# Hybrid encoder block: the first norm's second row tile in two parts, most rows scaled on GpSimd, and TensorE in a given order until the first half of the tokens is through

## The chip, the cores and the metric

The kernel runs on one core of a Trainium2 chip. The metric is the device time of one execution in microseconds (us), the median of three runs. The names of the engines in the profile: PE is TensorE (matmuls; PEld its weight loads), DVE is VectorE, ACT is ScalarE, POOL is GpSimd, SP is SyncE, which issues most of the loads. An `ACTq` or `SPq` is the part of an engine that issues DMAs.

## The reference

One layer of a streaming encoder over 512 tokens of 1024 features, in float32. What matters here is its beginning:

```python
def rmsnorm(x, g):
    var = jnp.mean(x * x, axis=-1, keepdims=True)
    return x * lax.rsqrt(var + EPS) * g

xn = rmsnorm(h, norm_mix_g)
u = xn @ w_in                               # 1024 x 7168
q, k, v, xr, gr, ga, gb = split(u)          # 1024 columns each
ya = chunked_band_attention(q, k, v) @ w_attn_out
xc = causal_depthwise_conv(xr)              # then the RG-LRU, times gelu(gr)
yb = ... @ w_rnn_out
mix = (sigmoid(ga + b) * ya + sigmoid(gb + b) * yb) @ w_o
h = h + mix;  h = h + SwiGLU(rmsnorm(h));  out = rmsnorm(h)
```

So every projection of `u` reads the normed rows `xn`, with tokens on the free axis of TensorE and features on the partitions.

## The kernel before

**Numbers.** TensorE multiplies in a format of reduced precision. To keep float32's precision, every operand is split into a high part and a low part (what is left of it), and a product is three matmuls into the same bank (`mm3`): high by high (L80), weights high by x low (L81), weights low by x high (L82). The order's names read out<-in; `whl_xr_0` holds the high and low parts of the weights of chunk xr, feature blocks 0 to 3, and `whl_xr_4` those of blocks 4 to 7. The high part of a weight tile is made by ACT (L672, L86), the low part by VectorE (L673, L87), from a raw tile (`raw_xr`) that SP loads. The tiles `whl` come from a pool of four buffers, so the tile of the fifth, `whl_ga_0`, takes the buffer of `whl_xr_0` when TensorE has read that for the last time.

**The first norm.** The 512 tokens lie in four row tiles x0 to x3 of 128 tokens. x0 and x1 are "half 0", x2 and x3 "half 1". For each half, `rstds` makes the sum of squares of the first tile on ACT, and of the second tile half on ACT (`low`, the columns 0 to 511) and half on VectorE (`high`, 512 to 1023), then the root on ACT and the reciprocal on VectorE. `scaled_first` and `scaled_rest` scale the rows into `xs_mix`: the low columns of both tiles on VectorE, later the high columns of the first tile on VectorE and those of the second on ACT. `turned(half, xs, jp)` does a pair of feature blocks jp and jp+1 (jp = 0, 2, 4, 6): four transposes on TensorE (128 tokens by 128 features each) into two PSUM tiles, `pt_mix_<jp>t` and `pt_mix_<jp>s`, from which ACT makes the high part of `xnT`, times the gain `gm` (L656), and VectorE the low part (L658).

**What runs in which order.** TensorE has nothing to do before half 0 is normed, and half 1 comes later. So the first two columns chunks, xr and gr, are multiplied for half 0 first (`first_half`: 2 chunks x 8 feature blocks x 2 column blocks x 3 matmuls of 128x256 = 96), then half 1 is transposed and its 96 matmuls follow, then ga and the rest with 512 tokens at a time. In the block around `scaled_first` the order of ACT, VectorE and GpSimd is the order of the code (`tc.manual_schedule`); TensorE's is chosen by a scheduler, and so is the order of all engines behind that block. Sixteen matmuls on zeros (`busy`, L478) run on TensorE while x comes in. GpSimd in that time issues loads of small vectors, later makes the low part of the gate weights `wrg` (L699) and copies the bias table (`ext`, L736, L737).

SP issues its loads in the order x0, x1, raw_xr_0, raw_xr_4, x2, x3, raw_gr_0, then the gate weights; an engine's loads use eight semaphores in turn, so a ninth load waits until the first has landed.

Of the kernel before, what the change touches and what calls it, by code (L numbers as in the profile page):

```python
# [42 lines left out]
def block_kernel(ctx: ExitStack, tc: tile.TileContext, x, norm_mix_g, w_in, b_merge, rel_table,  # L43
# [427 lines left out]
    for t in range(2):  # L471
        sp.dma_start(out=xt[t][:], in_=x[t * P:(t + 1) * P, :])
# [134 lines left out]
    low, high = slice(0, S), slice(S, D)  # L607

# [3 lines left out]
    def rstds(half):  # L612

        q = cp.tile([P, 4], F32, tag="ssq", bufs=4, name=f"ssq{half}")
        sd = cp.tile([P, 2], F32, tag="sd", bufs=4, name=f"sd_mix{half}")
        rs = cp.tile([P, 2], F32, tag="rs", bufs=4, name=f"rs_mix{half}")
        a, b = xt[2 * half], xt[2 * half + 1]
        junk = junk_of(nm, "junk", 1, f"a{half}")
        act.activation(junk[:], a[:], AF.Square, accum_out=q[:, 0:1])
        act.activation(sd[:, 0:1], q[:, 0:1], AF.Sqrt, bias=eps_t[:], scale=1.0 / D)  # L620
        dve.reciprocal(rs[:, 0:1], sd[:, 0:1])
        junk = junk_of(nm, "junk", 1, f"b{half}")
        act.activation(junk[:, low], b[:, low], AF.Square, accum_out=q[:, 1:2])
        junk = junk_of(qkp, "qk", 3, f"c{half}")
        dve.tensor_tensor_reduce(junk[:, high], b[:, high], b[:, high], 1.0 / D, EPS, ALU.mult, ALU.add, q[:, 2:3])
        act.activation(sd[:, 1:2], q[:, 1:2], AF.Sqrt, bias=q[:, 2:3], scale=1.0 / D)
        return sd, rs

    def scaled_rows(half, i, xs, rs, at, eng=None):
        dst, src = xs[i][:, at], xt[2 * half + i][:, at]  # L630
        if eng is act:
            act.activation(dst, src, AF.Copy, scale=rs[:, i:i + 1])
        else:
            dve.tensor_scalar(dst, src, rs[:, i:i + 1], None, ALU.mult)

    def scaled_first(half):

        xs = [nm.tile([P, D], F32, tag="xs", bufs=2, name=f"xs_mix{2 * half + i}") for i in range(2)]
        sd, rs = rstds(half)
        scaled_rows(half, 0, xs, rs, low)  # L640
        dve.reciprocal(rs[:, 1:2], sd[:, 1:2])
        scaled_rows(half, 1, xs, rs, low)
        return xs, rs

    def scaled_rest(half, xs, rs):
        scaled_rows(half, 0, xs, rs, high)
        scaled_rows(half, 1, xs, rs, high, act)

    def turned(half, xs, jp):

        pts = [ps.tile([P, 256], F32, tag=tag, bufs=2, name=f"pt_mix{half}_{jp}{tag}") for tag in "ts"]
        for i in range(2):
            for j in range(2):
                pe.transpose(pts[j][:, i * P:(i + 1) * P], xs[i][:, (jp + j) * P:(jp + j + 1) * P], ident[:])
        for j in range(2):
# [26 lines left out]
    def first_half(name, ks):  # L682
# [3 lines left out]
        for k in ks:  # L686
            for c in range(2):
                at = slice(c * P, (c + 1) * P)
                whl = made[index[name]]
                mm3(first[name, c][:, 0:256], whl(0, k, at), whl(1, k, at),  # L690
                    xnT[k][:, 0, 0:256], xnT[k][:, 1, 0:256], k == 0, k == KT - 1)
# [1067 lines left out]
```

## Time and profile before

| | |
|---|---|
| time, median of 3 runs | 844.44 us (844.41 to 850.82) |
| the profiled execution | 844.43 us, its span 842.6 us |
| mean granted clock of TensorE | 0.999 |
| busy: TensorE / VectorE / ACT / GpSimd | 834.4 / 659.3 / 517.4 / 160.2 us |
| first transpose of half 0 / first matmul of xr | 7.34 / 9.01 us |
| first matmul of gr, half 0 | 16.22 us |
| first transpose of half 1 / first matmul of xr, half 1 | 21.98 / 23.25 us |
| first matmul of xr with the feature blocks 4 to 7, half 1 | 30.07 us |
| first matmul that reads the gate weights (rg) | 46.90 us |

A row of the timeline reads: start, duration, engine, line, operation, out<-in, shape, count, and in brackets the idle time ahead of it and who ended it. A row of a group has the busy time and the mean duration in ns, then the idle time ahead. Matmuls are pipelined: their records overlap, and the distance between two starts, not a record's length, is what one costs.

### The profile page before, as it was taken

Reading aid. Unit: us, or ns where it says so; the run is one execution under the profiler, and the core shown is the slowest. Engines: PE = TensorE matmul, PEld = TensorE weight load, DVE = VectorE, ACT = ScalarE, POOL = GpSimd, SP = SyncE. Lnnn points to the kernel's source line nnn. Section 1 sums busy time; section 2 is a strip of 40 time slices with the busy share of each in tenths; the row PEclk is TensorE's granted clock in tenths of the full one; section 3 lists DMA queues with packets and bytes.
Section 4 is the critical chain, followed back from the end, with each engine's and each line's share of the span. In section 5 each row is a group of like instructions: output and inputs, shape, how many; then the busy total and the mean of one; then the engine's idle time right before and its main releaser. Section 6 shows DMA issues by size and latency. Waiting matters only on the chain.

```text
span 842.6 us, 11949 instructions
## 1 busy us (share of the span) xinstructions
PE 834.4 (99%) x4246; PEld 708.5 (84%) x4246; DVE 659.3 (78%) x958; ACT 517.4 (61%) x850; POOL 160.2 (19%) x219
## 2 busy tenths in 40 slices
PE   8999999999999999999999999999999999999997
PEld 6988888888888888888888888888888999988886
DVE  6688778887959878887568767889778878997784
ACT  7686848774356688878544557663765465455553
POOL 2502030221020043333211012005101321300000
PEclk9999999999999999999999999999999999999999
DMA  9566488653645455548458975455955576644442
GB/s 282 173 227 225 147 300 255 189 197 109 195 155 150 138 146 140 170 134 222 91 135 217 321 287 169 156 183 166 221 181 158 152 188 183 214 154 143 162 170 100
DMA packets 107323, 153.98 MB, mean 183 GB/s; under 512 B 8216, under 2 KB 66160, under 8 KB 106752
## 3 DMA queue, kind: packets, MB, share of 16 engines
q1 hardware_dynamic: 102304, 141.32, 51.8%
q0 software_dynamic: 3728, 8.96, 6.4%
q10 hardware_dynamic: 1232, 2.95, 0.9%
q8 instruction: 33, 0.54, 0.3%
q14 instruction: 26, 0.21, 0.1%
HBM read 139.53 MB, written 30.45 MB: 202 GB/s over the span
## 4 chain that ended last, share of the span: by engine, by line
PE 98%; DMA 1%; ACT 0%; DVE 0%; issue 0%; SPq 0%; ACTq 0%
PE fu_x L82 2%; PE fu_x L81 2%; PE fu_x L80 2%; PE o L1127 2%; PE fg_x L82 2%; PE fg_x L80 2%; PE fg_x L81 2%; PE pT L1107 2%; PE po_xr L81 2%; PE po_xr L80 2%; PE po_gb L80 2%; PE po_ga L80 2%; PE po_gr L80 2%; PE po_gr L82 2%; PE po_gr L81 2%; PE po_xr L82 2%
## 5 line engine op out<-in xcount | busy, mean ns | idle before, releaser
L1091 ACT ACTIVATE p<-p,m 128x128 f32<-128x128 f32 (+1 forms) x64 | 35.5, 555 | 9.7 <-DVE m L1090 9.3
L1096 POOL TENSOR_SCALAR p<-p,rl 128x128 f32<-128x128 f32 (+3 forms) x61 | 37.5, 629 | 16.9 <-DVE rl L1092 12.7
L1090 DVE CUSTOM_DVE_ANT_0 p<-s,bias 128x128 f32<-128x128 f32 (+1 forms) x64 | 28.7, 486 | 12.7 <-PE s L1082 10.7
L1348 POOL TENSOR_TENSOR sg<-sg,keep_fu_x 128x512 f32<-128x512 f32 x8 | 13.6, 1695 | 101.5 <-DVE keep_fu_x L1347 101.5
L87 DVE TENSOR_TENSOR whl_fu_w<-raw_fu_w,whl_fu_w 128x1024 fp32r<-128x1024 f32 (+1 forms) x18 | 23.4, 1307 | 9.2 <-ACT whl_fu_w L86 9.0
L87 DVE TENSOR_TENSOR pp<-pT,pp 128x384 fp32r<-128x384 f32 (+1 forms) x48 | 26.9, 595 | 2.0 <-ACT pp L86 1.8
L745 POOL MEMSET bias<- 64x64 f32 x16 | 2.3, 146 | 136.2 <-DMA bias<-ext_d 136.1
L87 DVE TENSOR_TENSOR whl_fu_t<-t_fu,whl_fu_t 128x1024 fp32r<-128x1024 f32 (+1 forms) x18 | 24.5, 1372 | 4.8 <-ACT whl_fu_t L86 4.7
L81 PE MATMUL po_xr<-xnT,whl_xr 128*128 128x512 f32 (+1 forms) x80 | 27.7, 353 | 0.0
L81 PE MATMUL po_gr<-xnT,whl_gr 128*128 128x512 f32 (+1 forms) x80 | 27.5, 347 | 0.0
L82 PE MATMUL po_gr<-xnT,whl_gr 128*128 128x512 f32 (+1 forms) x80 | 27.3, 347 | 0.0
L82 PE MATMUL po_xr<-xnT,whl_xr 128*128 128x512 f32 (+1 forms) x80 | 27.2, 347 | 0.0
L80 PE MATMUL po_gr<-xnT,whl_gr 128*128 128x512 f32 (+1 forms) x80 | 27.2, 347 | 0.0
L80 PE MATMUL po_xr<-xnT,whl_xr 128*128 128x512 f32 (+1 forms) x80 | 26.3, 351 | 0.4 <-ACT xnT L656 0.4
L86 ACT ACTIVATE whl_fu_w<-raw_fu_w 128x1024 fp32r<-128x1024 f32 (+1 forms) x18 | 17.7, 986 | 13.3 <-issue 7.6
L80 PE MATMUL po_q<-xnT,whl_qk 128*128 128x512 f32 x64 | 25.5, 398 | 0.0
L80 PE MATMUL po_k<-xnT,whl_qk 128*128 128x512 f32 x64 | 25.5, 398 | 0.0
L80 PE MATMUL po_ga<-xnT,whl_ga 128*128 128x512 f32 x64 | 25.4, 398 | 0.0
L80 PE MATMUL po_gb<-xnT,whl_gb 128*128 128x512 f32 x64 | 25.3, 395 | 0.0
L81 PE MATMUL po_q<-xnT,whl_qk 128*128 128x512 f32 x64 | 25.0, 390 | 0.0
L81 PE MATMUL po_ga<-xnT,whl_ga 128*128 128x512 f32 x64 | 25.0, 390 | 0.0
L81 PE MATMUL po_k<-xnT,whl_qk 128*128 128x512 f32 x64 | 25.0, 390 | 0.0
(689 smaller groups left out, 3089.1 us busy)
## 6 DMA issues: line engine op xcount, KB each, us to landing
raw_qk<-in_w_in_dram SPq DMA_DIRECT2D x32, 256.0 KB, 3.3
out_t<-in_w_ffn_out_dram SPq DMA_DIRECT2D x16, 512.0 KB, 5.5
raw_fu_w<-in_w_ffn_in_dram SPq DMA_DIRECT2D x16, 512.0 KB, 4.5
raw_fo<-in_w_ffn_out_dram SPq DMA_DIRECT2D x14, 512.0 KB, 4.3
raw_t<-out_t SPq DMA_DIRECT2D x24, 256.0 KB, 3.3
raw_xr<-in_w_in_dram SPq DMA_DIRECT2D x8, 512.0 KB, 5.8
raw_gr<-in_w_in_dram SPq DMA_DIRECT2D x8, 512.0 KB, 4.0
raw_ga<-in_w_in_dram SPq DMA_DIRECT2D x8, 512.0 KB, 4.9
```

The costliest lines, as they stand in the source:

```text
L80: pe.matmul(o, sh, mh, start=start, stop=False, skip_group_check=parts)
L81: pe.matmul(o, sh, ml, start=False, stop=False, skip_group_check=parts)
L82: pe.matmul(o, sl, mh, start=False, stop=stop, skip_group_check=parts)
L86: act.activation(hi, src, AF.Copy)
L87: dve.tensor_sub(lo, src, f(hi))
L745: pool.memset(b[64:128, 448:512], NEG)
L1090: dve.tensor_tensor_reduce(prob[qb][:], scs[qb][:, 0:w], bias[:, S - w:S], -1.0, 3e38, ALU.add, ALU.min, nmax[:, qb:qb + 1])
L1091: act.activation(prob[qb][:], prob[qb][:], AF.Exp, bias=nmax[:, qb:qb + 1], scale=-1.0, accum_out=lsum[:, qb:qb + 1])
L1096: eng.tensor_scalar(prob[qb][:], prob[qb][:], rl[:, qb:qb + 1], 1.0, ALU.mult, ALU.mult)
L1107: pe.transpose(pt[:, at * P:(at + 1) * P], prob[qb][:, kb * P:(kb + 1) * P], ident[:])
L1127: pe.matmul(po[:, S - n:S], st, pp[i][:, part, lo:lo + n], start=kb == 0 and part == 0, stop=kb == NT - 1 and part == 1)
L1348: (pool if keep and (unit != f_units[-1] or side) else dve).tensor_mul(o, o, keep_ if keep else bank)
```

## The change

1. The load of x0 is issued in two halves of 64 rows, one by SP and one by ACT, and that of x1 in two halves of 512 columns, both by SP.
2. `scaled` takes the place of `rstds`, `scaled_first` and `scaled_rest`. The second tile's squares: VectorE does the columns 0 to 511 ahead of the first tile's reciprocal and 512 to 767 behind it, ACT 768 to 1023. The rows: VectorE scales the columns 0 to 255 of the first tile and 0 to 511 (in two operations) of the second, GpSimd the rest in three operations; ACT scales none.
3. `gm` is copied on ACT ahead of the first weight split instead of behind it.
4. `turned` ends with the transposes; ACT's and VectorE's part is in `taken`, called later.
5. `first_half` goes over all high by high products of its feature blocks, then weights low by x high, then weights high by x low; before, each block had its three products in a row.
6. TensorE's order is the code's until half 0 is through, and pair 0 of half 1 is transposed ahead of the last feature block of gr.

```diff
@@ -468,8 +468,10 @@
-    for t in range(2):
-        sp.dma_start(out=xt[t][:], in_=x[t * P:(t + 1) * P, :])
+    for eng, rows in ((sp, slice(0, 64)), (act, slice(64, P))):
+        eng.dma_start(out=xt[0][rows, :], in_=x[rows, :])
+    for at in (slice(0, S), slice(S, D)):
+        sp.dma_start(out=xt[1][:, at], in_=x[P:2 * P, at])
...
@@ -604,47 +606,40 @@
         return sp2, sp4
 
 
-    low, high = slice(0, S), slice(S, D)
-
     def junk_of(pl, tag, bufs, name):
         return pl.tile([P, D], F32, tag=tag, bufs=bufs, name=f"junk_{name}")
 
-    def rstds(half):
-
+    def scaled(half):
+
+        xs = [nm.tile([P, D], F32, tag="xs", bufs=2, name=f"xs_mix{2 * half + i}") for i in range(2)]
         q = cp.tile([P, 4], F32, tag="ssq", bufs=4, name=f"ssq{half}")
         sd = cp.tile([P, 2], F32, tag="sd", bufs=4, name=f"sd_mix{half}")
         rs = cp.tile([P, 2], F32, tag="rs", bufs=4, name=f"rs_mix{half}")
         a, b = xt[2 * half], xt[2 * half + 1]
+
+        def rows(eng, i, at):
+            eng.tensor_scalar(xs[i][:, at], (a, b)[i][:, at], rs[:, i:i + 1], None, ALU.mult)
+
+        low, high, last = slice(0, S), slice(S, 768), slice(768, D)
+        one, two, rest = slice(0, 256), slice(256, S), slice(S, D)
         junk = junk_of(nm, "junk", 1, f"a{half}")
         act.activation(junk[:], a[:], AF.Square, accum_out=q[:, 0:1])
         act.activation(sd[:, 0:1], q[:, 0:1], AF.Sqrt, bias=eps_t[:], scale=1.0 / D)
+        junk = junk_of(nm, "junk", 1, f"b{half}")
+        act.activation(junk[:, last], b[:, last], AF.Square, accum_out=q[:, 1:2])
+        junk = junk_of(qkp, "qk", 3, f"c{half}")
+        dve.tensor_tensor_reduce(junk[:, low], b[:, low], b[:, low], 1.0 / D, EPS, ALU.mult, ALU.add, q[:, 2:3])
         dve.reciprocal(rs[:, 0:1], sd[:, 0:1])
-        junk = junk_of(nm, "junk", 1, f"b{half}")
-        act.activation(junk[:, low], b[:, low], AF.Square, accum_out=q[:, 1:2])
-        junk = junk_of(qkp, "qk", 3, f"c{half}")
-        dve.tensor_tensor_reduce(junk[:, high], b[:, high], b[:, high], 1.0 / D, EPS, ALU.mult, ALU.add, q[:, 2:3])
-        act.activation(sd[:, 1:2], q[:, 1:2], AF.Sqrt, bias=q[:, 2:3], scale=1.0 / D)
-        return sd, rs
-
-    def scaled_rows(half, i, xs, rs, at, eng=None):
-        dst, src = xs[i][:, at], xt[2 * half + i][:, at]
-        if eng is act:
-            act.activation(dst, src, AF.Copy, scale=rs[:, i:i + 1])
-        else:
-            dve.tensor_scalar(dst, src, rs[:, i:i + 1], None, ALU.mult)
-
-    def scaled_first(half):
-
-        xs = [nm.tile([P, D], F32, tag="xs", bufs=2, name=f"xs_mix{2 * half + i}") for i in range(2)]
-        sd, rs = rstds(half)
-        scaled_rows(half, 0, xs, rs, low)
+        dve.tensor_tensor_reduce(junk[:, high], b[:, high], b[:, high], 1.0 / D, q[:, 2:3], ALU.mult, ALU.add, q[:, 3:4])
+        act.activation(sd[:, 1:2], q[:, 1:2], AF.Sqrt, bias=q[:, 3:4], scale=1.0 / D)
+        rows(dve, 0, one)
+        rows(pool, 0, two)
+        rows(pool, 0, rest)
         dve.reciprocal(rs[:, 1:2], sd[:, 1:2])
-        scaled_rows(half, 1, xs, rs, low)
-        return xs, rs
-
-    def scaled_rest(half, xs, rs):
-        scaled_rows(half, 0, xs, rs, high)
-        scaled_rows(half, 1, xs, rs, high, act)
+        rows(dve, 1, one)
+        rows(dve, 1, two)
+        rows(pool, 1, rest)
+        return xs
 
     def turned(half, xs, jp):
 
@@ -652,6 +647,10 @@
         for i in range(2):
             for j in range(2):
                 pe.transpose(pts[j][:, i * P:(i + 1) * P], xs[i][:, (jp + j) * P:(jp + j + 1) * P], ident[:])
+        return half, jp, pts
+
+    def taken(half, jp, pts):
+
         for j in range(2):
             act.activation(part_of(jp + j, 0, half), pts[j][:], AF.Identity, scale=gm[:, jp + j:jp + j + 1])
         for j in range(2):
@@ -683,12 +682,13 @@
         for c in range(2):
             if (name, c) not in first:
                 first[name, c] = mm_tile(f"po_{name}_{c}")
-        for k in ks:
-            for c in range(2):
-                at = slice(c * P, (c + 1) * P)
-                whl = made[index[name]]
-                mm3(first[name, c][:, 0:256], whl(0, k, at), whl(1, k, at),
-                    xnT[k][:, 0, 0:256], xnT[k][:, 1, 0:256], k == 0, k == KT - 1)
+        whl = made[index[name]]
+        for sw, sx in ((0, 0), (1, 0), (0, 1)):
+            for k in ks:
+                for c in range(2):
+                    at = slice(c * P, (c + 1) * P)
+                    pe.matmul(first[name, c][:, 0:256], whl(sw, k, at), xnT[k][:, sx, 0:256],
+                              start=k == sw == sx == 0, stop=k == KT - 1 and sx == 1)
 
 
     wrg = rw2.tile([P, 2, 8, P], F32R, bufs=1, name="wrg")
@@ -699,36 +699,44 @@
         pool.tensor_sub(wrg[:, 1], raw, f(wrg[:, 0]))
 
     with tc.manual_schedule(engines={mybir.EngineType.Activation, mybir.EngineType.DVE, mybir.EngineType.Pool}):
-        xs, rs = scaled_first(0)
+        in_order = ExitStack()
+        in_order.enter_context(tc.manual_schedule(engines={mybir.EngineType.PE}))
+        xs = scaled(0)
+        act.copy(gm[:], gm_p[:, 0:8])
         xr0 = chunk_in_parts("xr0")
         xr0(0, 2, dve)
-        act.copy(gm[:], gm_p[:, 0:8])
-        turned(0, xs, 0)
-        first_half("xr0", range(0, 2))
-        scaled_rest(0, xs, rs)
-        xr0(2, 2, dve)
-        turned(0, xs, 2)
-        first_half("xr0", range(2, 4))
-        xr0(4, 2, dve)
-        turned(0, xs, 4)
-        first_half("xr0", range(4, 6))
-        gr0 = chunk_in_parts("gr0")
-        xr0(6, 2, dve)
-        turned(0, xs, 6)
-        first_half("xr0", range(6, 8))
+        pts = turned(0, xs, 0)
+        for k in range(0, KT, 2):
+            taken(*pts)
+            if k == 0:
+                pts = turned(0, xs, 2)
+                first_half("xr0", range(2))
+            elif k < KT - 2:
+                pts = turned(0, xs, k + 2)
+                first_half("xr0", range(k, k + 2))
+            else:
+                first_half("xr0", range(k, k + 2))
+            if k == 2:
+                gr0 = chunk_in_parts("gr0")
+            if k < KT - 2:
+                xr0(k + 2, 2, dve)
         gr0(0, 4, dve)
-        first_half("gr0", range(0, 4))
+        first_half("gr0", range(0, 2))
+        first_half("gr0", range(2, 4))
         gr0(4, 4, dve)
-        xs, rs = scaled_first(1)
+        xs = scaled(1)
         gate_weights()
-        turned(1, xs, 0)
-        first_half("gr0", range(4, 8))
-        scaled_rest(1, xs, rs)
-        turned(1, xs, 2)
+        first_half("gr0", range(4, 6))
+        first_half("gr0", range(6, 7))
+        pts = turned(1, xs, 0)
+        first_half("gr0", range(7, 8))
+        in_order.close()
+        taken(*pts)
+        taken(*turned(1, xs, 2))
         vectors()
         sp2, spm4 = softplus_neg()
-        turned(1, xs, 4)
-        turned(1, xs, 6)
+        taken(*turned(1, xs, 4))
+        taken(*turned(1, xs, 6))
 
 
     ext = nm.tile([HEADS, 640], F32, tag="junk", bufs=1, name="ext")
```

**The order on VectorE in the first norm**, from the reciprocal of the first tile on (`x_116` is x0, `x_117` is x1, `junk_c` takes squares that nobody reads; ISA is the sum of squares). Before:

```order
L621 RECIPROCAL rs_mix_189<-sd_mix_188 128x1
L625 ISA junk_c_196,ssq_187<-x_117 128x512
L625 ISA ssq_187 128x1
L634 TENSOR_SCALAR xs_mix_185<-x_116,rs_mix_189 128x512
L641 RECIPROCAL rs_mix_189<-sd_mix_188 128x1
L634 TENSOR_SCALAR xs_mix_186<-x_117,rs_mix_189 128x512
L673 TENSOR_TENSOR whl_xr_0_202<-raw_xr_0_152,whl_xr_0_202 128x512
```

After, with one sum ahead of the reciprocal:

```order
L631 ISA junk_c_199,ssq_191<-x_117 128x512
L631 ISA ssq_191 128x1
L632 RECIPROCAL rs_mix_193<-sd_mix_192 128x1
L633 ISA junk_c_199,ssq_191<-x_117,ssq_191 128x256
L633 ISA ssq_191 128x1
L621 TENSOR_SCALAR xs_mix_189<-x_116,rs_mix_193 128x256
L638 RECIPROCAL rs_mix_193<-sd_mix_192 128x1
L621 TENSOR_SCALAR xs_mix_190<-x_117,rs_mix_193 128x256 x2
L672 TENSOR_TENSOR whl_xr_0_212<-raw_xr_0_154,whl_xr_0_212 128x512
```

The squares of 512 columns moved ahead of the reciprocal, 256 stand behind it, and each scaling is 256 columns wide.

**The order on TensorE at the turn of the halves** (`xs_mix_339` and `xs_mix_340` before, `xs_mix_346` and `xs_mix_347` after are the scaled rows of x2 and x3). Before, the last two matmuls of gr, eight transposes and the first matmul of half 1:

```order
L81 MATMUL po_gr_1_310<-xnT,whl_gr_4_282 128x256
L82 MATMUL po_gr_1_310<-xnT,whl_gr_4_282 128x256
L654 MATMUL pt_mix_0t<-ident,xs_mix_339 128x128
L654 MATMUL pt_mix_0s<-ident,xs_mix_339 128x128
L654 MATMUL pt_mix_2t<-ident,xs_mix_339 128x128
L654 MATMUL pt_mix_2s<-ident,xs_mix_339 128x128
L654 MATMUL pt_mix_0t<-ident,xs_mix_340 128x128
L654 MATMUL pt_mix_0s<-ident,xs_mix_340 128x128
L654 MATMUL pt_mix_2t<-ident,xs_mix_340 128x128
L654 MATMUL pt_mix_2s<-ident,xs_mix_340 128x128
L80 MATMUL po_xr_0_217<-xnT,whl_xr_0_202 128x256
```

After, from pair 0's second transpose on, without the last two transposes of pair 2:

```order
L649 MATMUL pt_mix_0s<-ident,xs_mix_346 128x128
L649 MATMUL pt_mix_0t<-ident,xs_mix_347 128x128
L649 MATMUL pt_mix_0s<-ident,xs_mix_347 128x128
L690 MATMUL po_gr_0_316<-xnT,whl_gr_4_271 128x256
L690 MATMUL po_gr_1_317<-xnT,whl_gr_4_271 128x256
L690 MATMUL po_gr_0_316<-xnT,whl_gr_4_271 128x256
L690 MATMUL po_gr_1_317<-xnT,whl_gr_4_271 128x256
L690 MATMUL po_gr_0_316<-xnT,whl_gr_4_271 128x256
L690 MATMUL po_gr_1_317<-xnT,whl_gr_4_271 128x256
L649 MATMUL pt_mix_2t<-ident,xs_mix_346 128x128
L649 MATMUL pt_mix_2s<-ident,xs_mix_346 128x128
```

Six matmuls of gr moved between the transposes of pair 0 and those of pair 2.

**The order on VectorE behind the turn** (`sp_r` is a small vector of the recurrence, `whl_ga_0` and `whl_ga_4` are the first weights of the gate ga). Before:

```order
L583 RECIPROCAL sp_r<-sp_e_413 128x8
L658 SCALAR_TENSOR_TENSOR xnT<-pt_mix_4t,gm,xnT 128x256
L658 SCALAR_TENSOR_TENSOR xnT<-pt_mix_4s,gm,xnT 128x256
L658 SCALAR_TENSOR_TENSOR xnT<-pt_mix_6t,gm,xnT 128x256
L658 SCALAR_TENSOR_TENSOR xnT<-pt_mix_6s,gm,xnT 128x256
L87 TENSOR_TENSOR whl_ga_0_535<-raw_ga_0_536,whl_ga_0_535 128x1024
L87 TENSOR_TENSOR whl_ga_4_540<-raw_ga_4_541,whl_ga_4_540 128x1024
```

After:

```order
L585 RECIPROCAL sp_r<-sp_e_424 128x8
L87 TENSOR_TENSOR whl_ga_0_546<-raw_ga_0_547,whl_ga_0_546 128x1024
L657 SCALAR_TENSOR_TENSOR xnT<-pt_mix_4t,gm,xnT 128x256
L657 SCALAR_TENSOR_TENSOR xnT<-pt_mix_4s,gm,xnT 128x256
L657 SCALAR_TENSOR_TENSOR xnT<-pt_mix_6t,gm,xnT 128x256
L657 SCALAR_TENSOR_TENSOR xnT<-pt_mix_6s,gm,xnT 128x256
L87 TENSOR_TENSOR whl_ga_4_551<-raw_ga_4_552,whl_ga_4_551 128x1024
```

`whl_ga_0` moved ahead of the four low parts of `xnT`; on ACT its high part moved in the same way, ahead of the four high parts. On TensorE, between the last matmul that reads `whl_xr_0` and the first that reads `whl_xr_4` there now stand 15 rows: 11 matmuls of 128x256 and 4 transposes of pairs 4 and 6; before, there were 10 matmuls. Elsewhere the order of the program differs by some neighbours on ACT and VectorE only.

## The prediction

> **What bounds the kernel now.** I read the page's totals first, then the chain that ended last, then what TensorE (PE) waited for.
>
> ```profile
> span 842.6 us, 11949 instructions
> PE 834.4 (99%) x4246; PEld 708.5 (84%) x4246; DVE 659.3 (78%) x958; ACT 517.4 (61%) x850; POOL 160.2 (19%) x219
> PE 98%; DMA 1%; ACT 0%; DVE 0%; issue 0%; SPq 0%; ACTq 0%
> ```
>
> TensorE is busy 834.4 of 842.6 us, and 98% of the chain is its own. The change adds and removes no matmul, so it can only touch the 8.2 us in which TensorE is idle, and gaps of less than a tenth that overlapping records hide. The waits of TensorE are few:
>
> ```profile
> PE busy L478 <- DVE eps_t L484: 1.2, 1, 1.2
> PE pt_mix_0t L654 <- DVE xs_mix L634: 0.8, 2, 0.6
> PE po_xr L80 <- ACT xnT L656: 0.4, 2, 0.2
> ```
>
> The second and third belong to the first norm. The chain shows them in order (start, duration, what), first for the first 256 tokens, then at the turn to the other 256:
>
> ```profile
> 1.17 4.99 DMA x<-in_x_dram
> 6.18 0.72 ACT junk_b L623 x2
> 6.99 0.30 ACT sd_mix L626
> 7.31 0.17 DVE rs_mix L641
> 7.51 0.50 DVE xs_mix L634
> 8.05 0.34 PE pt_mix_0t L654
> 8.48 0.48 ACT xnT L656
> 9.01 0.50 PE po_xr L80 x2
> ...
> 22.73 0.48 ACT xnT L656
> 23.25 0.50 PE po_xr L80 x2
> ```
>
> The path to the first matmul at 9.01 is: the second row tile lands (1.17 + 4.99 = 6.16), sum of squares, root, reciprocal, scaling, transposes, ACT's copy. From 9.01 on TensorE runs nearly without a break. So four places count: the start, the stretch from 9.01 to the turn, the turn, and what is moved behind the turn.
>
> **Place 1, the start: -0.34 us if nothing contends.** VectorE's (DVE's) half of the sum of squares and its price, with a row of another two-input operation for the slope by width:
>
> ```profile
> 6.10 0.16 DVE L621 RECIPROCAL rs_mix<-sd_mix 128x1 f32<-128x1 f32 x1 [4.97 <-ACT sd_mix L620]
> 6.19 0.69 DVE L625 CUSTOM_DVE_ANT_0 junk_c<-x 128x512 f32<-128x512 f32 x1
> 15.00 1.23 DVE L673 TENSOR_TENSOR whl_gr<-raw_gr,whl_gr 128x1024 fp32r<-128x1024 f32 x1 [0.27 <-ACT whl_gr L672]
> ```
>
> Before, 512 columns are squared from 6.19 to 6.88, when the whole tile has landed. After, 512 columns are done ahead, on the part that lands first, and the last 256 follow the reciprocal, which ends at 6.10 + 0.16 = 6.26. With 0.69 at 512 columns and 1.23 at 1024, 256 are estimated at 0.69 - 0.27 = 0.42: the sum ends at 6.68, 0.20 earlier. The scaling of the second tile that the transposes need is now 256 columns instead of 512; 0.49 (7.51 to 8.00) falls to an estimated 0.35, between half and all of it. Together 0.34 earlier. From the scaled rows to the first matmul (8.00 to 9.01) I leave the 1.01 as it is. Bounds: 0 if x lands 0.34 later, 0.44 if the scaling halves.
>
> The two halves of the loads cost issue slots, not bytes:
>
> ```profile
> 0.73 0.86 SPq L472 DMA_DIRECT2D x<-in_x_dram  x2
> 13.92 1.05 ACT L672 ACTIVATE whl_gr<-raw_gr 128x1024 fp32r<-128x1024 f32 x1
> 17.33 1.05 ACT L619 ACTIVATE junk_a<-x 128x1024 f32<-128x1024 f32 x1
> ```
>
> SyncE (SP) issues one load in 0.43, so three instead of two put its later loads 0.43 back, and the half that ACT issues, and the wait for an earlier landing that the loads of x2, x3 and gr now have, hold them until about 4.6 to 6.2. What they bring is first used at 13.92 (gr) and 17.33 (x2). I cost this at nothing; if that cover were gone, it would cost at most what the loads slip, 2 to 3 us. How x0 and x1 land among each other is unknown; the nearest row is the issue time, so +-0.4 is my bound. The Trainium skill, page "DMA: Bandwidth & Descriptors", section "Issuing engines are not separate DMA queues", says that DMAs from several engines run on the same 16 DMA engines and that spreading them saves issue time only. By it x0 would land no earlier than by the 0.43 of one issue, which is inside the bound taken.
>
> **GpSimd (POOL) against VectorE.** What GpSimd's scaling costs, and what the two engines do to each other, these rows show:
>
> ```profile
> L1096 POOL TENSOR_SCALAR p<-p,rl 128x512 f32<-128x512 f32 x13 | 9.0, 693 | 0.0
> L1096 POOL TENSOR_SCALAR p<-p,rl 128x256 f32<-128x256 f32 x16 | 9.0, 562 | 0.0
> 6.80 0.48 DVE L634 TENSOR_SCALAR xs_mix<-x,rs_mix 128x512 f32<-128x512 f32 x1
> 19.47 0.50 POOL L736 COPY ext<-tab 16x384 f32<-16x384 f32 x1 [13.53 <-ACT junk_b L623]
> 19.50 0.75 DVE L634 TENSOR_SCALAR xs_mix<-x,rs_mix 128x512 f32<-128x512 f32 x1
> 29.11 0.24 POOL L592 TENSOR_SCALAR sp_p<-sp_p 128x8 f32<-128x8 f32 x1
> 30.33 1.18 POOL L592 TENSOR_SCALAR sp_p<-sp_p 128x8 f32<-128x8 f32 x1
> 30.19 2.40 DVE L87 TENSOR_TENSOR whl_ga<-raw_ga,whl_ga 128x1024 fp32r<-128x1024 f32 x2 [0.44 <-ACT whl_ga L86]
> ```
>
> Three scalings on GpSimd take 0.56 + 0.69 + 0.69 = 1.94: from 6.26 on, to 8.2 at best. The columns from 512 on are transposed for pair 4, behind the twelve matmuls of pair 0, at 9.01 + 12 x 0.12 = 10.4, so 2 us cover them. But the same scaling took VectorE 0.75 instead of 0.48 when a GpSimd copy began just before it, and an operation of eight columns took GpSimd 1.18 instead of 0.24 beside VectorE's two-input operation. One holds up the other. At 6.26 VectorE goes straight from the reciprocal to its 256 columns of squares, so GpSimd waits there; next both want to go, VectorE for 256 columns of the first tile. Bounds for VectorE's delay on the path: 0 (GpSimd waits, as at 30.33) and 0.94, the 1.18 less the 0.24 of the waiting row. I take the row nearest in kind, 0.75 - 0.48 = **+0.27**. Place 1 then gives -0.34 + 0.27 = -0.07.
>
> The Trainium skill, page "SBUF — State Buffer", section "Who interferes with whom", speaks against the change: GpSimd and VectorE's second port pair are one exclusive lock, and a VectorE operation with two SBUF inputs, or a scaling in a two-port mode, and a GpSimd operation that reads SBUF block each other for a whole instruction. The 1.18 agrees; by the rule in full, place 1 is the rival B below.
>
> **Place 2, 9.01 to the turn: -0.49 us.** The stretch by windows (busy us and count of each engine), and its marks:
>
> ```profile
> 9.01:16.22 7.21, 7.19 (x57) 6.82 (x57) 6.71 (x13) 5.73 (x12) 0.00 (x0) 1.00 1.07 312
> 16.22 0.28 PE L80 MATMUL po_gr<-xnT,whl_gr 128*128 128x256 f32 x1
> 21.86 0.29 PE L82 MATMUL po_gr<-xnT,whl_gr 128*128 128x256 f32 x1
> 21.98 0.27 PE L654 MATMUL pt_mix_0t<-ident,xs_mix 128*128 128x128 f32 x1
> 22.42 0.27 PE L654 MATMUL pt_mix_0t<-ident,xs_mix 128*128 128x128 f32 x1
> ```
>
> A matmul of 256 columns follows the one before after 0.12 (21.86 to 21.98), a transpose after 0.11 (four in the 0.44 from 21.98 to 22.42). From 16.22 to 21.98 there are 48 matmuls: 48 x 0.12 = 5.76, no loss. From 9.01 to 16.22 there are 48 and 8 transposes: 5.76 + 8 x 0.107 = 6.62 of 7.21, so 0.59 is lost, though its busy time reads 7.19, since a waiting matmul's record is drawn longer. Here VectorE (6.71 of 7.21) is as full as TensorE. After, a pair's four products high by high and the four with the weights' low parts come first, 8 x 0.12 = 0.96 before the low part of xnT is read, and ACT and VectorE lose one scaling each (0.72 and 0.48). Per pair VectorE then works about 0.6 + 2 x 0.4 = 1.4 against 12 x 0.12 + 4 x 0.107 = 1.87 on TensorE. I leave 0.1 of the loss and take -0.49; the bounds are 0 and -0.59.
>
> **Place 3, the turn: -0.41 us.** 21.98 to 23.25 is 1.27, of which 8 transposes are 0.86; 0.41 is the wait for ACT's copy. After, pair 0 is transposed first and six gr matmuls (0.72) and pair 2's four transposes (0.43) stand between it and its first use: 1.15, against the 0.83 that passed between the second token tile's transpose into pair 0 and its first use (22.42 to 23.25). The wait goes. It needs the scaled rows 0.8 us sooner; ACT squares 256 columns fewer and VectorE scales fewer, so I see 0.2 to spare. Bounds: -0.41 and 0.
>
> **Place 4, behind the turn: +0.76 us, a new wait.** In the order of ACT and VectorE the split of whl_ga_0 now stands ahead of xnT of pairs 4 and 6; before it stood behind them.
>
> ```profile
> 28.36 0.48 DVE L658 SCALAR_TENSOR_TENSOR xnT<-pt_mix_4s,gm,xnT 128x256 fp32r<-128x256 f32 x1
> 28.76 0.28 PE L82 MATMUL po_xr<-xnT,whl_xr 128*128 128x256 f32 x1
> 29.10 2.23 ACT L86 ACTIVATE whl_ga<-raw_ga 128x1024 fp32r<-128x1024 f32 x2
> 30.07 0.40 PE L80 MATMUL po_xr<-xnT,whl_xr 128*128 128x256 f32 x2
> ```
>
> whl_ga_0 takes the buffer of whl_xr_0, so ACT starts it 0.34 after the last matmul that reads whl_xr_0 (28.76 to 29.10), VectorE's low part 1.09 later (30.19), which takes 2.40 / 2 = 1.20, and xnT's low part of pair 4 then 0.48: 3.11 after that matmul. In the new order 15 rows of TensorE (11 matmuls, 4 transposes) and four products high by high stand between: 0.12 + 11 x 0.12 + 4 x 0.107 + 4 x 0.12 = 2.35. TensorE waits 3.11 - 2.35 = 0.76, with the queue of all its later work behind it. Below it could be 0 (nothing stood there before), above 1.2 if ACT's copies also come late.
>
> **The sum**, against the profiled execution of 844.43 us (span 842.6 and 1.8 around it; the median of the runs is 844.44): -0.07 - 0.49 - 0.41 + 0.76 = -0.21, so 844.22, said as **844.2**.
>
> **Rivals.**
> - **A, forecast, 0.45:** gains at places 2 and 3, given back at place 4: 844.2, of its own 843.9 to 844.6.
> - **B, slower, 0.22:** the two engines hold each other for whole instructions at the start. GpSimd takes its turn between VectorE's, so the second tile's 256 columns come 0.94 late instead of 0.27: -0.21 + 0.67 = +0.46, 844.9. It decides as soon as VectorE loses over 0.27 + 0.21 = 0.48. For it the 1.18 speaks, against it that VectorE got away with 0.27 where GpSimd was first.
> - **C, faster, 0.16:** the wait behind the turn isn't there, because TensorE comes later to the spot, or ACT sooner: 844.2 - 0.76 = 843.5; and 843.2 with GpSimd waiting each time (another 0.27). Against it: the split can't start before its buffer is free.
> - **D, 0.12:** the split loads don't bring x sooner where it is needed, x1 0.4 later or sooner: 843.8 to 844.6. In this case the change doesn't do what it says at the start.
> - The rest, 0.05, is a load that comes late by more, or an order far behind.
>
> **The range.** 843.1 to 845.2 holds A, D, most of B (844.9 and its 0.3 of spread) and most of C. About 1%, 8.4 us, is what a measurement of this kernel can tell from no change, and the whole idle time of TensorE is 8.2: within 1% 0.96, faster and slower 0.02 each, since only a late load or a disturbed order could do it.
>
> **What the new profile would show.** The first po_xr matmul at 8.6 to 9.0 (B: 9.3 to 9.6); from it to the first half-1 transpose about 0.1 over the count of rows; no wait of po_xr for xnT at the turn; and a wait of 0.5 to 0.9 of po_xr L81 for VectorE's xnT near 31, behind whl_ga_0. VectorE's scaling rows longer than 0.35 beside GpSimd's are B. If the last wait is missing, C holds; if the span moves by more than 0.8 from 842.6, my sum is wrong.

## The result, and the profile after

The changed kernel takes 846.08 us, the median of 14 runs (845.39 to 847.94), against 844.50 for the kernel before. The ratio, taken over the single runs and not from the medians, is 1.0016, its 95% interval 1.0009 to 1.0023. It is slower by 1.6 us; the forecast was 844.2, range 843.1 to 845.2. Its profiled execution took 846.15, 1.72 more than that of before. The page shows about the same totals as before, with 8.9 us more on GpSimd:

```profile
span 844.3 us, 11970 instructions
PE 834.2 (99%) x4246; PEld 708.4 (84%) x4246; DVE 661.0 (78%) x962; ACT 515.2 (61%) x848; POOL 169.1 (20%) x225
```

TensorE's waits have changed place. Those of po_xr for ACT's xnT, one of them at the turn, are gone. The wait for the first scaled rows is longer, 2.0 us, and two waits for VectorE are new (pt_mix_2t at the turn, po_xr behind it):

```profile
PE pt_mix_0t L649 <- DVE xs_mix L621: 2.0, 1, 2.0
PE busy L480 <- DVE eps_t L486: 1.2, 1, 1.2
PE pt_mix_2t L649 <- DVE xs_mix L621: 0.6, 1, 0.6
PE po_xr L81 <- DVE xnT L657: 0.6, 1, 0.6
```

The chain, from the load of x to the end of the last new wait:

```profile
0.73 4.89 DMA x<-in_x_dram
5.71 1.16 ACT junk_a L626 x2
...
21.65 2.33 DVE xs_mix L621 x2
24.02 0.33 PE pt_mix_2t L649
...
29.46 1.07 ACT whl_ga L86
30.56 1.23 DVE whl_ga L87
31.78 0.41 DVE xnT L657
```

x now lands at 5.62 (0.73 + 4.89), over 1 us later than the 4.59 at which ACT began on it before. Four marks of TensorE cut the time up to the gate matmuls (rg) into the prediction's four places. In the kernel after they are these rows of its timeline:

```profile
9.82 0.39 PE L690 MATMUL po_xr<-xnT,whl_xr 128*128 128x256 f32 x1
16.87 0.28 PE L690 MATMUL po_gr<-xnT,whl_gr 128*128 128x256 f32 x1
24.21 0.48 PE L80 MATMUL po_xr<-xnT,whl_xr 128*128 128x256 f32 x2
48.62 0.73 PE L808 MATMUL rg<-xch,wrg 64*128 64x512 f32 x4
```

The same marks of every profiled execution, as differences (start of the first row of each kind; before, rg starts at 46.83, while the 46.90 of the table ahead of the prediction is its start in the chain). The medians stand with the median of before on the same chip:

| kernel | first xr | xr to gr | gr to half 1's xr | from there to rg | rg | median | before |
|---|---|---|---|---|---|---|---|
| before | 9.01 | 7.21 | 7.03 | 23.58 | 46.83 | 844.50 | |
| after | 9.82 | 7.05 | 7.34 | 24.41 | 48.62 | 846.08 | 844.50 |
| e1 after, x loaded whole | 9.21 | 7.05 | 6.55 | 24.42 | 47.23 | 844.98 | 844.55 |
| e2 before, split loads | 10.00 | 7.22 | 7.04 | 23.58 | 47.84 | 845.62 | 844.55 |
| e3 after, x0 whole | 9.48 | 6.84 | 6.65 | 24.41 | 47.38 | 846.44 | 844.55 |
| e4 after, x1 whole | 10.38 | 7.02 | 6.55 | 24.39 | 48.34 | 845.91 | 844.55 |
| e5 as e4, both halves of x0 on SP | 10.00 | 7.07 | 6.63 | 24.41 | 48.11 | (846.25) | 844.66 |
| e6 after, whl_ga behind xnT | 9.99 | 7.04 | 6.56 | 23.55 | 47.14 | 845.18 | 844.66 |
| e7 as e1, whl_ga behind xnT | 9.29 | 7.05 | 6.55 | 23.54 | 46.43 | 844.47 | 844.66 |
| e8 as e1, no scaling on GpSimd | 9.53 | 6.85 | 6.55 | 23.56 | 46.49 | 844.06 | 844.66 |
| e9 before, new orders only | 9.04 | 6.82 | 6.55 | 23.57 | 45.98 | 843.87 | 844.68 |
| e10 before, products by kind only | 8.99 | 6.62 | 7.27 | 23.58 | 46.46 | 844.36 | 844.68 |
| e11 as e8, idle GpSimd scalings beside | 9.41 | 6.99 | 7.26 | 24.11 | 47.77 | (845.49) | 844.68 |
| e12 as e7, two operations on GpSimd | 9.41 | 6.85 | 9.29 | 23.55 | 49.10 | 847.81 | 844.68 |

(In brackets: one run. In e10 two matmuls of xr stand behind the first of gr, see there.) For after, the four differences to before are +0.81, -0.16, +0.31 and +0.83; they sum to +1.79, which is what rg is late (48.62 - 46.83) and about what the span has grown (1.7). So the whole loss lies ahead of rg.

### The profile page after: what moved, and what is told of

Read it like the earlier page. It is cut to its first block, busy times and chain, and to the rows that moved or that the text cites. A ratio compares the mean times of both kernels' runs of the same rounds, so it can differ in the third digit from the quotient of the medians.

```text
span 844.3 us, 11970 instructions
## 1 busy us (share of the span) xinstructions
PE 834.2 (99%) x4246; PEld 708.4 (84%) x4246; DVE 661.0 (78%) x962; ACT 515.2 (61%) x848; POOL 169.1 (20%) x225
## 4 chain that ended last, share of the span: by engine, by line
PE 96%; DVE 2%; DMA 1%; ACT 1%; issue 0%; ACTq 0%; DVEq 0%
PE fu_x L81 2%; PE fu_x L80 2%; PE fu_x L82 2%; PE o L1135 2%; PE fg_x L82 2%; PE fg_x L80 2%; PE fg_x L81 2%; PE pT L1115 2%; PE po_gb L80 2%; PE po_ga L80 2%; PE po_q L80 2%; PE po_k L80 2%; PE po_q L81 2%; PE po_ga L81 2%; PE po_gb L81 2%; PE po_ya L82 2%
## 5 line engine op out<-in xcount | busy, mean ns | idle before, releaser
L80 PE MATMUL po_q<-xnT,whl_qk 128*128 128x512 f32 x64 | 25.5, 398 | 0.0
L80 PE MATMUL po_ga<-xnT,whl_ga 128*128 128x512 f32 x64 | 25.5, 398 | 0.0
L80 PE MATMUL po_gb<-xnT,whl_gb 128*128 128x512 f32 x64 | 25.3, 395 | 0.0
L81 PE MATMUL po_ga<-xnT,whl_ga 128*128 128x512 f32 x64 | 25.0, 390 | 0.0
L81 PE MATMUL po_q<-xnT,whl_qk 128*128 128x512 f32 x64 | 25.0, 390 | 0.0
L81 PE MATMUL po_k<-xnT,whl_qk 128*128 128x512 f32 x64 | 25.0, 390 | 0.0
L81 PE MATMUL po_gb<-xnT,whl_gb 128*128 128x512 f32 x64 | 24.9, 390 | 0.0
L80 PE MATMUL po_yb<-rnn,whl_yb 128*128 128x512 f32 x64 | 24.9, 390 | 0.0
L82 PE MATMUL po_q<-xnT,whl_qk 128*128 128x512 f32 x64 | 24.9, 390 | 0.0
L82 PE MATMUL po_ga<-xnT,whl_ga 128*128 128x512 f32 x64 | 24.9, 390 | 0.0
L82 PE MATMUL po_yb<-rnn,whl_yb 128*128 128x512 f32 x64 | 24.9, 390 | 0.0
L82 PE MATMUL po_ya<-aT,whl_ya 128*128 128x512 f32 x64 | 24.9, 389 | 0.0
```

The lines of the kernel that those rows point to most:

```text
L80: pe.matmul(o, sh, mh, start=start, stop=False, skip_group_check=parts)
L81: pe.matmul(o, sh, ml, start=False, stop=False, skip_group_check=parts)
L82: pe.matmul(o, sl, mh, start=False, stop=stop, skip_group_check=parts)
```

## The experiments

Three theories for the loss: **L**, the split loads bring x late; **K**, GpSimd and VectorE hold each other up; **O**, the place of whl_ga_0.

**e1, whole loads.** Edit to the changed kernel:

```diff
-    for eng, rows in ((sp, slice(0, 64)), (act, slice(64, P))):
-        eng.dma_start(out=xt[0][rows, :], in_=x[rows, :])
-    for at in (slice(0, S), slice(S, D)):
-        sp.dma_start(out=xt[1][:, at], in_=x[P:2 * P, at])
+    sp.dma_start(out=xt[0][:], in_=x[0:P, :])
+    sp.dma_start(out=xt[1][:], in_=x[P:2 * P, :])
```

> The changed kernel with x0 and x1 loaded whole on SP again, as before. Theory L (the split loads bring x0 1.1 us late, 5.69 for 4.57): x0 lands near 4.6, the first matmul of xr near 9.1 for 9.82, the median falls by 0.6 to 0.9 us to about 845.3. Rival K (GpSimd and VectorE hold each other up, and the start is bound by that): x0 lands early but the first matmul stays within 0.3 of 9.82 and the median within 0.3 of 846.1.

Measured 844.98, ratio to before 1.0008 (0.9999 to 1.0018), 1.1 under the changed kernel. x0 is there at 4.5, as before:

```profile
4.53 1.06 ACT L624 ACTIVATE junk_a<-x 128x1024 f32<-128x1024 f32 x1 [1.69 <-DMA x<-in_x_dram]
```

L holds. The first matmul comes 0.61 earlier, yet at 9.21 it is still 0.20 later than before. Another 0.79 comes back at the turn (6.55 for 7.34).

**e2, the split loads alone**, the same lines put into the kernel before.

> The kernel before with only the four split loads of the change. Theory L: x0 lands near 5.7, x1 near 7, the first matmul of xr near 9.9 for 9.01, and the median rises by 0.8 to 1.1 us to about 845.4. Rival K: the loads alone cost under 0.3 us.

845.62, ratio 1.0012 (1.0003 to 1.0022): +1.07, with the first matmul at 10.00 and every later difference as before. The loads alone cost as much as they gave back in e1.

**e3 and e4, one half of the edit each.** In e3 x0 is whole, in e4 x1.

> The changed kernel with x0 whole on SP, x1 still in two column halves. If the half of x0 on the second queue is what makes x0 late: x0 lands near 4.6 and the start is that of the whole loads or up to 0.3 earlier, median near 845.2. If it is x1's packets of half the size that slow everything: x0 lands near 5.2 or later and raw_xr stays 1 us late, median near 845.8.

> The changed kernel with x0 in two row halves on SP and ACT, x1 whole on SP. If the row halves on two queues are the cause: x0 lands near 5.6, the first matmul stays near 9.8, median near 846. If x1's column halves are: x0 lands near 4.6 to 4.9 and the median falls to about 845.3.

In e3 x0 is there at 4.49, in e4 at 5.76: it is x0's row halves that make x0 late. But x1's column halves have a price too: in e3 the first matmul comes at 9.48, 0.27 later than in e1, where up to 0.3 earlier was expected. ACT can square the last 256 columns only at 6.88, where the whole tile landed at 6.16 in the kernel before, and the load behind x, raw_xr, is late as well (the same split starts at 7.46 before):

```profile
6.88 0.42 ACT L628 ACTIVATE junk_b<-x 128x256 f32<-128x256 f32 x1 [0.91 <-DMA x<-in_x_dram]
8.24 0.63 ACT L670 ACTIVATE whl_xr<-raw_xr 128x512 fp32r<-128x512 f32 x1 [0.30 <-DMA raw_xr<-in_w_in_dram]
```

The chain to that first matmul goes through raw_xr. x1's scaled rows are level with it: they are ready at 8.47, and from there to 9.48 pass the same 1.01 as before.

In e4 the first matmul comes at 10.38, where about 9.8 was expected: x1, whole but issued behind the half of x0, is there only at 7.2.

The medians are 846.44 (e3, ratio 1.0023, 1.0011 to 1.0034) and 845.91 (e4, 1.0017, 1.0008 to 1.0026). e3's was 1.2 above what was expected, though its profiled run, 844.92, was its fastest; its other runs lose up to 2.7 us in a place that this profile does not show.

**e5, both row halves on one queue**, x1 whole.

```diff
-    for eng, rows in ((sp, slice(0, 64)), (act, slice(64, P))):
+    for eng, rows in ((sp, slice(0, 64)), (sp, slice(64, P))):
```

> The changed kernel with both row halves of x0 issued by SP, one behind the other, x1 whole on SP. If the second queue makes x0 late (its packets and those of x1 and raw_xr share the engines): x0 lands near 4.6 to 4.9. If the height of 64 rows does, whatever the queue: x0 lands near 5.5 as in the kernel with one half on each.

```profile
0.73 1.22 SPq L472 DMA_DIRECT2D x<-in_x_dram  x2
5.60 1.06 ACT L625 ACTIVATE junk_a<-x 128x1024 f32<-128x1024 f32 x1 [2.76 <-DMA x<-in_x_dram]
```

x0 is late without a second queue too, so the cut by rows is enough; but the two ways of issuing it are late for different parts. On one queue much of it is the issue: two halves take SP 1.22 where one whole tile takes 0.43 (0.86 for two, before), so the second half is issued at 1.4, where x0 went out whole at 0.73. On two queues both halves are issued at 0.73, and the one from SP takes 4.89 to land, against 3.8 for the whole tile before. And in the changed kernel the DMA engines, though as busy, move less. These are the windows from 3.5 to 5.5 us, their last two columns the busy share of the DMA engines and GB/s, first of the kernel before and then of the changed one:

```profile
3.50:4.50 1.00, 1.00 (x3) 0.30 (x2) 0.00 (x0) 0.00 (x0) 1.00 (x3) 1.00 0.97 391
4.50:5.50 1.00, 1.00 (x5) 0.45 (x4) 0.00 (x0) 0.91 (x1) 1.00 (x3) 1.00 0.99 367
```

```profile
3.50:4.50 1.00, 1.00 (x4) 0.35 (x3) 0.00 (x0) 0.12 (x1) 1.00 (x3) 1.00 0.99 218
4.50:5.50 1.00, 1.00 (x7) 0.47 (x5) 0.00 (x0) 0.00 (x0) 1.00 (x3) 1.00 1.03 225
```

391 and 367 GB/s fall to 218 and 225. The Trainium skill, page "SBUF — State Buffer", section "Can I just issue two DMAs to hit both halves?", says that the ports are chosen by the span of partitions of a single transfer, that only a transfer over all 128 partitions reaches all of them, and that two transfers to the two halves at once serialize. The 218 and 225 against 391 and 367 agree with it, but do not show it alone: e3, which has no transfer of 64 rows, moves 255 and 304 in the same windows, against 414 and 340 in e1. The prediction weighed another sentence, on queues, and not this one. What in the cut slows the transfer stays open.

**e6 and e7, whl_ga behind xnT.** One line holds the order, e6 in the changed kernel and e7 in e1:

```diff
         taken(*turned(1, xs, 6))
+        prefetch(index["ga0"] + 1)
```

> The changed kernel, with the split of whl_ga_0 and whl_ga_4 held behind the last xnT of half 1, as before. Theory O (the order of whl_ga_0 makes TensorE wait): no wait of po_xr L81 for xnT, first rg 0.6 to 0.8 earlier than 48.62, median near 845.3. Rival: the wait of TensorE moves elsewhere (pair 4's transposes come as late), median within 0.3 of 846.1.

> Whole loads of x0 and x1 and whl_ga behind xnT; GpSimd's scaling and TensorE's order as changed. If the loads and the place of whl_ga carry the loss: first rg near 46.4 for 46.83 before, median near 844.1, 0.4 under before. If GpSimd's hold on VectorE costs more than the rest brings: 844.6 or more.

e6: 845.18 (ratio to before 1.0008, 0.9998 to 1.0017), 0.9 under the changed kernel; the stretch behind the turn falls from 24.41 to 23.55. The wait of po_xr for VectorE's xnT is missing in its list:

```profile
PE pt_mix_0t L649 <- DVE xs_mix L621: 1.3, 1, 1.3
PE busy L480 <- DVE eps_t L486: 1.2, 1, 1.2
```

O is shown. e7 gives 844.47 (ratio 0.9999, 0.9989 to 1.0008), 0.4 above what was expected, although its rg stands at the expected 46.43: its runs scatter from 843.72 to 846.82, and the profiled one, the slowest, has a wait far behind the change:

```profile
PE fg_x L82 <- DVE whl_fg_t L87: 2.1, 1, 2.1
```

Why such a late wait comes in some executions of these kernels was not tried.

**e8, no scaling on GpSimd.** e1, with the rows scaled as in the kernel before. The two new lines stand in a function `more` that runs where `scaled_rest` did:

```diff
-        rows(dve, 0, one)
-        rows(pool, 0, two)
-        rows(pool, 0, rest)
+        rows(dve, 0, low)
...
-        rows(dve, 1, one)
-        rows(dve, 1, two)
-        rows(pool, 1, rest)
+        rows(dve, 1, low)
...
+            rows(dve, 0, rest)
+            act.activation(xs[1][:, rest], b[:, rest], AF.Copy, scale=rs[:, 1:2])
```

> Whole loads; rows scaled by VectorE and ACT as before (low columns at once, high columns behind the first pair), the other parts as changed; whl_ga stands behind xnT in this kernel's order. Theory K (GpSimd and VectorE hold each other for whole operations): VectorE's scalings take 0.35 to 0.5 each, the first matmul comes near 8.9, half 1's first near 22.4, median near 843.7. Rival: without GpSimd, ACT and VectorE are late with the high columns, TensorE waits in pairs 4 and 6, and the median is 844.1 or more.

844.06, ratio 0.9995 (0.9986 to 1.0005); the first matmul at 9.53 and half 1's at 22.93 missed the expected 8.9 and 22.4. VectorE's scalings of 512 columns take 0.48 and 0.49 again, but the marks from gr on are those of e7 within 0.06 (the first matmul is 0.24 later, 0.17 of it because ACT could begin on x0 at 4.78 instead of 4.61). So at the start GpSimd's work and its hold on VectorE cancel, and K isn't what makes the start late. That is the new split of the squares: with whole loads, VectorE's 512 columns begin when x1 lands and 256 more follow (0.69 + 0.48), where it did 512 before:

```profile
6.18 0.69 DVE L629 CUSTOM_DVE_ANT_0 junk_c<-x 128x512 f32<-128x512 f32 x1 [5.04 <-DMA x<-in_x_dram]
6.91 0.48 DVE L631 CUSTOM_DVE_ANT_0 junk_c<-x,ssq 128x256 f32<-128x256 f32 x1
```

**e9, the orders alone.** The changed kernel with loads and norm of before (`rstds`, `scaled_first`, `scaled_rest`); `taken`, `first_half`, TensorE's order and the place of `gm` as changed.

> The kernel before with only the order parts of the change: products of a feature pair by kind, TensorE in the code's order until the first half is through, pair 0 of half 1 ahead of gr's last block, gm ahead of the first split. Loads, sums of squares and scaling as before; whl_ga stands behind xnT. If the order parts bring what the prediction's places 2 and 3 say: first matmul near 9.0, first gr near 15.9, half 1's first near 22.4, first rg near 46.0 for 46.83, median 0.7 to 0.9 under before. Rival: without GpSimd's help ACT and VectorE are late in the first pairs and the gain stays at 0.4.

843.87 (843.56 to 844.48, 11 runs) against 844.68, ratio 0.9992 (0.9983 to 1.0001). Its rg at 45.98 is 0.85 earlier than before, as expected, and no wait at the turn is left. It is the fastest version here: 2.2 under the changed kernel, and 0.81 under the kernel before, with an interval that just reaches no change.

**e10, the products by kind alone**, in the kernel before.

```diff
-                mm3(first[name, c][:, 0:256], whl(0, k, at), whl(1, k, at),
-                    xnT[k][:, 0, 0:256], xnT[k][:, 1, 0:256], k == 0, k == KT - 1)
+        for sw, sx in ((0, 0), (1, 0), (0, 1)):
...
+                    pe.matmul(first[name, c][:, 0:256], whl(sw, k, at), xnT[k][:, sx, 0:256],
+                              start=k == sw == sx == 0, stop=k == KT - 1 and sx == 1)
```

> The kernel before with only the products of a feature pair by kind (high by high, low by high, high by low), TensorE's order left to the scheduler. Place 2 of the prediction alone: the stretch from the first xr to the first gr falls from 7.21 to about 6.8, and the median by 0.3 to 0.5. Rival: the stretch is bound by VectorE (6.71 busy of 7.21) and stays within 0.1.

844.36, 0.32 less (ratio 0.9999, 0.9990 to 1.0008, so not told apart by the runs alone). The mark of xr to gr falls to 6.62, but not over the same matmuls: here TensorE's order puts eight matmuls of gr ahead of the last two of xr.

```profile
15.61 1.12 PE L691 MATMUL po_gr<-xnT,whl_gr 128*128 128x256 f32 x8
16.57 0.40 PE L691 MATMUL po_xr<-xnT,whl_xr 128*128 128x256 f32 x2
```

With these two (2 x 0.12) the stretch is 6.86 and the next one 7.03, as before. So the products by kind win 0.35 of the 0.59 that was lost, near the 6.8 expected.

**e11, idle GpSimd scalings beside e8**, and **e12, another form of GpSimd's scaling in e7.** e11 adds three GpSimd scalings of each half into a tile that nobody reads; e12 multiplies by 1.0 as a second operation:

```diff
-            eng.tensor_scalar(xs[i][:, at], (a, b)[i][:, at], rs[:, i:i + 1], None, ALU.mult)
+            two_ops = (1.0, ALU.mult, ALU.mult) if eng is pool else (None, ALU.mult)
+            eng.tensor_scalar(xs[i][:, at], (a, b)[i][:, at], rs[:, i:i + 1], *two_ops)
```

> The kernel of whole loads without GpSimd's scaling, and beside it three GpSimd scalings of 256, 256 and 512 columns of each half into a tile that nobody reads. Theory K: VectorE's scalings of 512 columns, 0.48 and 0.49 without, take about 1 us each beside GpSimd's, the first matmul comes 0.4 to 0.9 later than 9.53, GpSimd's 512 take 1.5. If they don't hold each other: durations and marks as without, within 0.1.

> Whole loads and whl_ga behind xnT as in the run of that name, GpSimd's scaling written with a second multiplication by 1.0, as the softmax's scaling is, whose 512 columns took 0.69. If the form sets GpSimd's price: its 512 columns take about 0.7 for 1.55, VectorE's second scalings fall from 1.05 to about 0.6, the first matmul comes near 9.0 for 9.29, pair 4 does not wait, median 0.3 to 0.5 under that run. If it is the operands or VectorE: 1.5 as before and the same median.

e11 missed at the start: GpSimd's 512 columns took 1.58, as expected, but VectorE's two scalings 0.69 and 0.49, and the first matmul came at 9.41, no later than without. At the turn they took 0.80 and 0.49 and the stretch 7.26 for e8's 6.55, though not by GpSimd alone, since ACT's split of the second gr tile also began 0.88 later in this execution (17.13 for 16.25). The hold came behind the turn, where VectorE's next scaling stood beside GpSimd's last one and the gate weights' subtraction:

```profile
24.20 3.27 DVE L619 TENSOR_SCALAR xs_mix<-x,rs_mix 128x512 f32<-128x512 f32 x1
24.78 2.40 POOL L700 TENSOR_TENSOR wrg<-wrg_raw,wrg 128x1024 fp32r<-128x1024 f32 x1
```

e12 halved GpSimd's price as expected (0.71 for 512 columns) and yet took 847.81 (ratio 1.0040, 1.0026 to 1.0053), 3.3 more than e7, since VectorE's scaling of x3 now began beside GpSimd's scalings and ended with that subtraction, which came earlier:

```profile
7.55 0.71 POOL L620 TENSOR_SCALAR xs_mix<-x,rs_mix 128x512 f32<-128x512 f32 x1
...
20.23 3.91 DVE L620 TENSOR_SCALAR xs_mix<-x,rs_mix 128x256 f32<-128x256 f32 x1
21.67 2.33 POOL L698 TENSOR_TENSOR wrg<-wrg_raw,wrg 128x1024 fp32r<-128x1024 f32 x1
24.20 0.33 PE L648 MATMUL pt_mix_0t<-ident,xs_mix 128*128 128x128 f32 x1 [2.52 <-DVE xs_mix L620]
```

256 columns that take VectorE 0.35 alone took 3.91 and ended at 24.14, just behind GpSimd's operation (21.67 + 2.33 = 24.00), and TensorE waited 2.52. That GpSimd can hold VectorE up is shown; what it costs is set by what GpSimd happens to run and by how soon TensorE needs the rows.

## Why the prediction was wrong, point by point

- **Place 1 is the step that failed**: -0.07 forecast, +0.81 measured. Between the forecast of -0.21 and the +1.79 of the marks lie 2.00: 0.88 here, 0.33 at place 2, 0.72 at place 3 and 0.07 at place 4. The prediction took the landing of x as that of before, with a bound of +-0.4, and looked only at issue time. x0's row halves put it 0.8 to 1.2 late (ACT begins on it at 5.4 to 5.8 in e2, e4, e5 and e6, for 4.59) and x1's last columns come 0.7 late (e3). Case D, in which the loads don't bring x sooner, had the mechanism, but stopped at 0.4. The estimates of VectorE's pieces held: 256 columns of squares 0.48 (0.42 forecast), 256 scaled 0.35 (0.35). But the gain of 0.34 was not there even with whole loads (9.21 in e1, 9.29 in e7): it needs the first 512 columns of x1 at 5.4 (their squares take 0.69 and have to be done when the reciprocal starts at 6.10), and the rest on time. No row showed that; in e3 the first half came at 5.7.
- **The later loads, put at nothing**: the prediction had the loads behind x covered until 13.92 and 17.33. It left out raw_xr, which ACT waited for in the kernel before already, and the second tile of gr. Both came later in the changed kernel (each row of before, then of after):

```profile
7.46 0.63 ACT L672 ACTIVATE whl_xr<-raw_xr 128x512 fp32r<-128x512 f32 x1 [0.18 <-DMA raw_xr<-in_w_in_dram]
8.61 0.63 ACT L671 ACTIVATE whl_xr<-raw_xr 128x512 fp32r<-128x512 f32 x1 [0.33 <-DMA raw_xr<-in_w_in_dram]
16.37 1.06 ACT L672 ACTIVATE whl_gr<-raw_gr 128x1024 fp32r<-128x1024 f32 x1 [1.40 <-DMA raw_gr<-in_w_in_dram]
17.28 1.06 ACT L671 ACTIVATE whl_gr<-raw_gr 128x1024 fp32r<-128x1024 f32 x1 [1.41 <-DMA raw_gr<-in_w_in_dram]
```

  What raw_xr cost alone can't be told, since x came late with it. The second pair puts the norm of half 1, which stands behind that split on ACT and VectorE, 0.9 later; its price shows at place 3.
- **Cost of GpSimd's scaling**: 1.94 forecast for three, 4.31 measured at the start. The term was priced from the softmax's scaling, which has two operations; these have one:

```profile
7.48 1.15 POOL L621 TENSOR_SCALAR xs_mix<-x,rs_mix 128x256 f32<-128x256 f32 x1 [1.55 <-DVE rs_mix L632]
8.63 1.62 POOL L621 TENSOR_SCALAR xs_mix<-x,rs_mix 128x512 f32<-128x512 f32 x1
10.22 1.57 POOL L621 TENSOR_SCALAR xs_mix<-x,rs_mix 128x512 f32<-128x512 f32 x1
```

  The last ends at 11.79, and so pair 4's second transposes stand at 11.85 instead of right behind 11.59. The "2 us of cover" were gone.
- **Place 2**: -0.49 forecast, -0.16 measured. The mechanism was right and its size too high: the order gives -0.35 by itself (e10, with the two late matmuls counted), -0.36 in e8 and -0.39 in e9, so 0.2 or more of the loss stays where 0.1 was allowed. In the changed kernel GpSimd's late rows take another 0.2 back.
- **Place 3**: -0.41 forecast. Six of the kernels with this order show 6.55 or 6.56, -0.48, so the order does what the sum said. The profiled execution of the changed kernel shows +0.31 instead, for two reasons together. One is a hold that the sum had only at the start: behind GpSimd's scaling VectorE's third scaling took 2.01.

```profile
21.18 1.10 POOL L621 TENSOR_SCALAR xs_mix<-x,rs_mix 128x256 f32<-128x256 f32 x1
21.65 0.38 DVE L621 TENSOR_SCALAR xs_mix<-x,rs_mix 128x256 f32<-128x256 f32 x1
21.95 2.01 DVE L621 TENSOR_SCALAR xs_mix<-x,rs_mix 128x256 f32<-128x256 f32 x1
```

  In e1, e6 and e7, with the same instructions, the two took 1.41 together and TensorE did not wait, so this part need not come in every execution; only one of the changed kernel was profiled. The other is the late norm of half 1. In e1, where the second gr tile is not late, the third scaling ended at 21.97 and pair 2's second transposes began at 22.67, so 0.70 was to spare; in e6, with the split loads, it ended at 23.25 for 23.46. The 0.87 that the hold took beyond the 1.14 of those runs met 0.2 of cover.
- **Place 4**: +0.76 forecast, +0.83 measured in the stretch, the wait at the row that was named (po_xr L81 for VectorE's xnT, at 32.23), and 0.86 to 0.88 taken away by e6 and e7.
- **Case B** had the right sign and mechanism for the wrong place: the hold cost nothing that counts at the start (e8 against e7), and 0.8 at the turn in one execution, together with the late norm. That its 844.9 lies nearer to the result than the forecast is luck.

By the medians, each taken against the kernel before on its own chip, the loss is: loads 1.15 (to e1), the place of whl_ga 0.62 (e1 to e7; 1.06 by e6), the GpSimd rows 0.41 (e7 to e8) and the new split of the squares 0.21 (e8 to e9); against it stand the orders, 0.81 gained (e9). They add up to the 1.58 measured, but each run's interval is about 0.8 either way, so single parts, those of 0.21 and 0.41 above all, are not clear of noise. By rg in the profiled executions the same steps are 1.39, 0.80, -0.06 and 0.51, against 0.85: there the GpSimd rows cost nothing once the loads are whole, and the squares cost more.

## What to carry to other kernels

Before a tile's load is cut, ask what the cut does to the transfer and not only to its issue: of two loads of half the rows the later one arrived after the time of the whole, and the loads behind came late with it. When a part of a change is a gain and another a loss of the same size, the sum tells nothing; marks of the bounding engine, stage by stage, told most of them apart in one profile each, where medians needed many runs. But a mark compares two kernels only if the same instructions stand ahead of it, as e10 shows. A duration borrowed from another line is only as good as its form: same engine, same shape and same operation count.

## What was not expected of the hardware

- GpSimd's scaling of 512 columns by a column of factors took 1.55 to 1.86 with one operation and 0.68 to 0.72 with a second one, a multiplication by 1.0 (256 columns: 0.93 to 1.28, and 0.59 to 0.69).
- GpSimd can hold a 256-column scaling of VectorE from 0.35 to 3.91. The Trainium skill, page "SBUF — State Buffer", section "Who interferes with whom", has, for a VectorE operation in a two-port mode, the second to issue blocked in full until the first is done. The 3.91, which ended 0.14 behind GpSimd's subtraction, agrees if it waited for three operations of GpSimd in a row; but in the changed kernel VectorE's scaling at 21.65 took 0.38 in the middle of one of GpSimd's (21.18 to 22.28), and in e3 VectorE's three scalings at the start took 0.35 each beside GpSimd's. So not every overlap blocks, and which does isn't settled here.
- A load of 64 rows of 4 KB took 0.58 to issue as SP's first load, against 0.38 to 0.42 for 128 rows. This is not a price by rows alone: the 128 rows of x1 behind such halves took 0.59 (e5) and 0.81 (e4).
